# Four raw weight buffers for the whole kernel, and the first gates in bytes that are free during mLSTM: a two-layer mixer trunk on one core

## The chip, the core and the metric

The kernel runs on 1 core of one Trainium2 chip. The metric is the device time of one execution in microseconds (us). The engines are named as in the profile: PE (matmul), PEld (its weight loads), DVE (VectorE), ACT (ScalarE), POOL (GpSimd) and SP (SyncE, which issues nearly all transfers of this kernel).

## The reference

A trunk of two layers works on 768 tokens (256 context and 512 latent) of width 1024, all in float32. Cut to what matters here, one layer is:

```python
hx = modulate(rms_norm(x, ln1), shift, scale)        # the same for the context
px = split_in(hx @ w_in + b_in)                      # 12 mixer parts and 3 * 1024 gate columns
a, b, c = token_mixers(px[:12])                      # HGRN2, mLSTM, RG-LRU, both directions
g = sigmoid(px[12])                                  # (tokens, 3, 1024)
merged = sum(g[n] * (branch[n] @ w_branch[n]) for n in range(3))
x = x + mod2 * (merged @ w_out)
x = x + mod5 * swiglu(modulate(rms_norm(x, ln2), ...), w_ffn_in, w_ffn_out)
```

The modulation vectors come from `silu(c) @ w_ada + b_ada`. The context stream runs through the merge and the FFN in the first layer only, so the second layer (L1) has outputs of 512 tokens and the first (L0) of 768.

## The kernel before

**Precision and panels.** Every large matmul is made of three: a weight panel of 128 x 1024 raw float32 is loaded (`ld`, always on SP), ACT copies it to a rounded high part `wh` (line 195), DVE subtracts to get the low part `wl` (line 197), and PE multiplies wh by the high and low parts of the activations and wl by the high part. `wload` does this for all phases. The raw panels rotate through a tag `w` with 2 buffers, `wh` and `wl` through 3 each, in the pool `wp` that lives for the whole kernel. In the merge and FFN phase `panel` gives every second panel a raw buffer from another tag, `wx`, with 2 buffers in that phase's own pool, so that panels alternate between `wx` and `w`. The loads of the modulation weights (`ada_steps`, 80 of them, 512 KB each) also rotate through `w`.

**Phases.** Memory is used in phases, each with a pool laid over the bytes of the one before: `stp` (start: modulation weights, tokens, the first norm), then for each layer `M0`/`M1` (the mixers) and `B0`/`B1` (merge, output projection, FFN). The order of first request, or an explicit list (`M_ORDER`), sets the addresses of the tags in a pool. A tile waits for the users of those earlier tiles that lay on its own bytes.

**Mixer phase.** Per layer: value projections `v_half`, four `hgrn` heads, four `lru` blocks, the mLSTM gates (names `L0mg`, `L1mg`), and `mlstm(0)` and `mlstm(1)` (names `L0ml`, `L1ml`). One `mlstm` has four projections (PE line 370), a prelude (transposes, the weighted keys, the chunk states, lines 927 to 959) and a loop over the output chunks, six in L0 and four in L1. One chunk is a chain: a transfer and DVE line 971, ACT exp (line 973), PE line 977, DVE line 980, PE lines 987 and 989, then ACT and DVE lines 992 to 997. After the loop, `head_norm_out` normalises and transposes (PE line 626), and the result is stored to DRAM.

**Merge.** `gates(br, m, tiles)` multiplies the layer's input by two blocks of 128 gate columns (two panels, PE line 1032, name `L0br_acc`) and writes tanh of it (ACT line 1051) into two tiles. In L0 such a pair has 96 matmuls and takes four PSUM buffers, in L1 48 and two; the tag `acc` has four. Branch 0 comes first: four pairs of gates go to the tags `ex` and `hid`, then the mixer results are loaded back (`zt`, 2 buffers), split (`bh`, 8 buffers, lines 1069 and 1070) and multiplied by `w_branch`. Branches 2 and 1 follow, each with one pair of gates ahead of its branch matmuls, in the tag `gt` with 4 buffers:

```python
gts = gates(br, 0, [B("gt") for _ in range(2)]) if n_ else []
for m in range(0, NK, 2):
    gcur = gts if n_ else mg[m:m + 2]
```

**Order.** Each engine has one queue, in an order that is fixed when the program is built, from priorities (roughly the order of the program text) and from what is expected to be ready. Panel loads and splits have a raised priority (`hoist`) after the first two heads; PE can therefore run a later phase's matmuls between those of a chain, if their panels and PSUM buffers are there.

Of the kernel before, what the change touches and what calls it, by code (L numbers as in the profile page):

```python
# [8 lines left out]
F32 = mybir.dt.float32  # L9
# [8 lines left out]
NK = 8  # L18
CTX = 256
LAT = 512  # L20
T = CTX + LAT
# [12 lines left out]
LEVELS = (1, 2, 4, 8, 16, 32, 64)  # L34
BUFS = {
# [3 lines left out]
}  # L39
M_ORDER = (("v", 516), ("z", T), ("o", T), ("kt", T), ("ks", 384), ("F", T), ("sd", T), ("th", T), ("q", T), ("K", T), ("Q", T), ("P", 384), ("col", 384))  # L40
HOIST = 4000


# [1 line left out]
def trunk_kernel(ctx: ExitStack, tc: tile.TileContext, a: dict, out: bass.AP):  # L45
    nc = tc.nc
    PSUM = bass.MemoryType.PSUM
    const = ctx.enter_context(tc.tile_pool(name="const", bufs=1))
    hp = ctx.enter_context(tc.tile_pool(name="hp", bufs=16))
    wp = ctx.enter_context(tc.tile_pool(name="wp", bufs=2))  # L50
# [8 lines left out]
    def nm(p):  # L59
        n_names[0] += 1  # L60
        return f"{part[0]}{p}{n_names[0]}"
# [3 lines left out]
    def S(tag, n=T, dt=F32, p=128):  # L65
        return pool[0].tile([p, n], dt, tag=tag, name=nm(tag), bufs=BUFS[tag])

    def phase(name, order=()):
        st = ExitStack()
        pool[0] = st.enter_context(tc.tile_pool(name=name, bufs=1, reuse_waits="tile"))  # L70
        for tag, n in order:
            S(tag, n)
        return st
# [28 lines left out]
    def ld(o, i):  # L102
        nc.sync.dma_start(o, i)

    stp = phase("stp")
    ii, jj, xr = [S("ij", 128, I32) for _ in range(3)]
    G.iota(ii, pattern=[[0, 128]], base=0, channel_multiplier=1)
    G.iota(jj, pattern=[[1, 128]], base=0, channel_multiplier=0)
    ident = const.tile([128, 128], F32, name="ident")
    V.tensor_tensor(ident, ii, jj, op=OP.is_equal)  # L110
    ones = const.tile([128, 1], F32, name="ones")
    V.memset(ones, 1.0)
    crow = const.tile([16, 128], F32, name="crow")
    ld(crow[0:8], a["c"].rearrange("b (k p) -> (b k) p", p=128))
    ld(crow[8:16], a["c_ctx"].rearrange("(k p) -> k p", p=128))
    tokst, awt = [], {}
# [7 lines left out]
    def ada_src(l, s, j):  # L124
        return a["w_ada"][l][s * 256:(s + 1) * 256, j * 512:(j + 1) * 512].rearrange("(k p) c -> p k c", p=128)
# [68 lines left out]
    def split_w(w, n, wh, wl, low=True):  # L194
        ACT.activation(wh[:, :n], w[:, :n], AF.Copy)  # L195
        if low:
            V.tensor_tensor(wl[:, :n], w[:, :n], wh[:, :n].bitcast(F32), op=OP.subtract)  # L197

    WN = 1088

    def wload(src, r0, nk, c0, ncol, extra=None, wl=None, low=True, w=None):
        with tc.high_priority(hoist[0]):
            w = w or wp.tile([128, WN], F32, tag="w", name=nm("w"), bufs=2)
            wh = wp.tile([128, WN], F32R, tag="wh", name=nm("wh"), bufs=3)
            if wl is None:
                wl = wp.tile([128, WN], F32R, tag="wl", name=nm("wl"), bufs=3)
            cw = ncol + (extra[1] if extra else 0)
            n = nk * cw
            v = w[:, :n].rearrange("p (k c) -> p k c", k=nk)
            ld(v[:, :, :ncol], src[r0:r0 + nk * 128, c0:c0 + ncol].rearrange("(k p) c -> p k c", p=128))  # L210
            if extra:
                ld(v[:, :, ncol:], src[r0:r0 + nk * 128, extra[0]:extra[0] + extra[1]].rearrange("(k p) c -> p k c", p=128))
            split_w(w, n, wh, wl, low)
        return (wh[:, :n].rearrange("p (k c) -> p k c", k=nk), wl[:, :n].rearrange("p (k c) -> p k c", k=nk))
# [22 lines left out]
    def ada_acc(ac, kk, wv):  # L237
        for i in range(len(ac)):
            if kk == 0:
                V.tensor_scalar(ac[i], wv, csk[:, kk, i:i + 1], None, op0=OP.mult)  # L240
            else:
                V.scalar_tensor_tensor(ac[i], wv, csk[:, kk, i:i + 1], ac[i], op0=OP.mult, op1=OP.add)  # L242
# [10 lines left out]
    def ada_steps(l, js):  # L253
        for j in js:
            nv = 2 if l == 0 or j < 4 else 1
            ac = None
            for s in range(4):
                was, part[0] = part[0], f"ada{l}_{j}_"
                w = wp.tile([128, WN], F32, tag="w", name=nm("w"), bufs=2)
                wv = w[:, :1024].rearrange("p (k c) -> p k c", k=2)  # L260
                with tc.high_priority(HOIST):
                    ld(wv, ada_src(l, s, j))
                if s == 0:
                    ac = [S("ny", 512) for _ in range(nv)]
                with tc.high_priority(HOIST):
                    for k in range(2):
                        ada_acc(ac, 2 * s + k, wv[:, k, :])
                if s == 3:
                    ada_reduce(l, j, ac)
                part[0] = was  # L270
                yield
# [254 lines left out]
    for c in LEVELS:  # L526
        lt = S("lt", 128)
# [14 lines left out]
    def hbcol(l, c0):  # L542
        i = c0 // 128 if c0 < 4096 else 32 + (c0 - 4112) // 128
        return halfb[l][:, i:i + 1]
# [3 lines left out]
    def layer(l, hh, hl):  # L548
# [4 lines left out]
        no = T - t0  # L553
# [19 lines left out]

        mpool = phase(f"M{l}", M_ORDER)
        rst = S("rst", T, p=64)
# [7 lines left out]
        vb = S("vb", 512)  # L583
        ld(vb, bass.AP(tensor=a["b_in"].tensor, offset=a["b_in"][l, O_V:O_V + 512].offset, ap=[[0, 128], [1, 512]]))
        vbm = S("vbm", 528)
# [416 lines left out]
            mlstm(p)  # L1002

        mpool.close()
        bpool = phase(f"B{l}")
        XO = t0

        def B(tag, dt=F32):
            return S(tag, no, dt)

        turn = [0]

        def panel(src, r0, nk, c0, wl=None, low=True):
            turn[0] += 1
            return wload(src, r0, nk, c0, 256, wl=wl, low=low, w=S("wx", 1024) if turn[0] % 2 else None)

        def dense2(panels, ah, al, groups, ao=0, mid=None):
            nks = [p[0].shape[1] for p in panels]
# [22 lines left out]
        def kpanels(src, r0, nks, c0, wls=(None, None), low=True):  # L1041
            out_, r = [], r0
            for nk, wl in zip(nks, wls):
                out_.append(panel(src, r, nk, c0, wl, low))
                r += nk * 128
            return out_

        def gates(br, m, gts_):
            col = O_GATE + br * D + m * 128
            for mm, ps, off, n in dense2(kpanels(w_in, 0, (4, 4), col), hh, hl, OG):  # L1050
                ACT.activation(gts_[mm][:, off - XO:off - XO + n], ps, AF.Tanh, scale=0.5, bias=hbcol(l, col + mm * 128))
            return gts_
# [3 lines left out]
            filler = ada_steps(0, range(4, 10))  # L1056
        part[0] = f"L{l}br0_"
        mg = [None] * NK
        for m in (6, 0, 2, 4):
            mg[m], mg[m + 1] = gates(0, m, [B("ex" if m == 6 else "hid") for _ in range(2)])  # L1060
        mh, mlo = [], []
        for n_, (br, zs) in enumerate(((0, za), (2, zc), (1, zb))):
            part[0] = f"L{l}br{br}_"
            bh, bl = [], []
            for i in range(4):
                z = B("zt")
                ld(z, zs[i][:, OT])
                zh, zl = B("bh", F32R), B("bh", F32R)
                ACT.activation(zh, z, AF.Copy)
                V.tensor_tensor(zl, z, zh.bitcast(F32), op=OP.subtract)  # L1070
                bh.append(zh)
                bl.append(zl)
            gts = gates(br, 0, [B("gt") for _ in range(2)]) if n_ else []
            for m in range(0, NK, 2):
                gcur = gts if n_ else mg[m:m + 2]
                for mm, ps, off, n in dense2([panel(a["w_branch"][l, br], 0, 4, m * 128)], bh, bl, OG, ao=XO):
                    gt = gcur[mm]
                    sl = slice(off - XO, off - XO + n)
                    V.scalar_tensor_tensor(gt[:, sl], gt[:, sl], 1.0, ps, op0=OP.add, op1=OP.mult)  # L1079
                    if n_:  # L1080
                        V.tensor_tensor(mg[m + mm][:, sl], mg[m + mm][:, sl], gt[:, sl], op=OP.add)
                if n_ == 2:
                    for i in (m, m + 1):
                        h_, l_ = B("hid", F32R), B("hid", F32R)
                        ACT.activation(h_, mg[i], AF.Copy, scale=0.5)
                        V.scalar_tensor_tensor(l_, mg[i], 0.5, h_.bitcast(F32), op0=OP.mult, op1=OP.subtract)
                        mh.append(h_)
                        mlo.append(l_)
                        mg[i] = None
                next(filler, None)  # L1090
                next(filler, None)
                if n_ and m + 2 < NK:
                    gts = gates(br, m + 2, [B("gt") for _ in range(2)])
        for _ in filler:
            pass

# [18 lines left out]
        xn = xs if l == 0 else [S("xn", 512) for _ in range(NK)]  # L1115
# [13 lines left out]
        for off, n in (GA, GB):  # L1129
            st = Stat(n, no)  # L1130
            for m0 in range(0, NK, 2):
                for mm, ps, _, _ in dense2(kpanels(a["w_out"][l], 0, (4, 4), m0 * 128), mh, mlo, ((off, n),), ao=XO):
                    m = m0 + mm
# [14 lines left out]
        hid = {}  # L1148
# [66 lines left out]
        for off, n in (GA, GB):  # L1215
# [29 lines left out]
            else:  # L1245
# [5 lines left out]
                for c in range(2):  # L1251
                    cb_ = (off - 256) // GR + 16 * c
                    for hf in range(2):
                        o = og[c][hf]
# [40 lines left out]
```

## Time and profile before

| | us |
|---|---|
| median of 3 runs | 2728.51 |
| lowest and highest | 2722.21 and 2735.47 |
| the profiled execution, own time | 2732.03 |
| its span | 2730.3 |
| PE busy in the span | 2577.0 |

The span is what the trace covers; 1.7 us of the execution's own time lie outside it. The granted TensorE clock averaged 0.962 of full speed. Times in the rows below count from the span's start, and line numbers are those of the kernel before.

### The profile page before, as it was taken

The page shows a single profiled execution, that of the slowest core. Times are in us where ns is not written, and L with a number is a line of the kernel's source. Part 1 is how long each engine was busy: PE and PEld are TensorE (multiplying, and loading weights), DVE is VectorE, ACT ScalarE, POOL GpSimd, SP SyncE. Part 2 cuts the span into 40 slices and gives each one's busy share as a digit, 9 for nine tenths or more (in the row PEclk, how much of TensorE's full clock was granted, in tenths as well). Part 3 has the DMA queues.
Part 4 walks back from the last instruction along what each step waited for, and adds up shares of the span by engine and source line. Part 5 has one row for each costly group of instructions (what it writes and reads, how often), then busy time and mean ns, then how long its engine had stood idle before and what let it go on. Part 6 is the DMA issues. An engine that isn't in the chain of part 4 may idle for free.

```text
span 2730.3 us, 35992 instructions
## 1 busy us (share of the span) xinstructions
PE 2577.0 (94%) x14415; PEld 2209.6 (81%) x14415; DVE 1583.0 (58%) x3023; ACT 956.5 (35%) x1468; POOL 12.0 (0%) x44
## 2 busy tenths in 40 slices
PE   6999999967999999999999989999897999999998
PEld 3999878756888888888888879987775888888887
DVE  6676796452655558645545366687853445743435
ACT  3434593212122343212212245348521333422223
POOL 0000000000000000000000000000000000000000
PEclk9999999958999999999999989999996999999999
DMA  6224243216545434424434144645343555423323
GB/s 218 55 41 53 45 69 63 59 43 139 127 113 117 119 122 134 131 90 142 131 92 140 61 110 62 58 58 68 51 83 71 132 101 148 136 95 95 99 89 112
DMA packets 270168, 264.42 MB, mean 97 GB/s; under 512 B 16136, under 2 KB 233616, under 8 KB 270000
## 3 DMA queue, kind: packets, MB, share of 16 engines
q1 hardware_dynamic: 269424, 261.06, 40.4%
q8 instruction: 114, 1.87, 0.3%
q10 hardware_dynamic: 576, 1.05, 0.1%
q14 instruction: 54, 0.44, 0.1%
HBM read 249.91 MB, written 12.16 MB: 96 GB/s over the span
## 4 chain that ended last, share of the span: by engine, by line
PE 73%; DVE 11%; DMA 9%; ACT 4%; issue 2%; SPq 0%; ACTq 0%; DVEq 0%
PE L1ffn_acc L1032 13%; PE L0ffn_acc L1032 13%; PE L0br_acc L1032 10%; PE L1br_acc L1032 6%; DMA ada_w<-in_w_ada_dram 4%; PE L0hg_acc L370 4%; PE L1hg_acc L370 3%; PE L0out_acc L1032 2%; PE L0lru_acc L370 2%; DVE ada_ny L242 2%; PE L0ml_acc L370 2%; PE L0hg_pl L693 2%; PE L1ml_acc L370 1%; PE L1mg_acc L480 1%; PE L1hg_pl L693 1%
## 5 line engine op out<-in xcount | busy, mean ns | idle before, releaser
L1032 PE MATMUL L0ffn_acc<-L0out_h,L0ffn_wh 128*128 128x256 f32 (+1 forms) x1408 | 348.6, 339 | 9.1 <-DVE L0ffn_gt L1160 4.5
L1032 PEld LDWEIGHTS L0ffn_acc<-L0out_h,L0ffn_wh 128*128 128x128 f32 x1408 | 241.2, 190 | 41.7 <-DVE L0ffn_gt L1160 5.8
L1032 PE MATMUL L0ffn_acc<-L0out_h,L0ffn_wl 128*128 128x512 f32 (+1 forms) x704 | 236.5, 336 | 0.0
L242 DVE SCALAR_TENSOR_TENSOR ada_ny<-ada_w,csk,ada_ny 128x512 f32<-128x512 f32 x224 | 158.2, 748 | 126.2 <-DMA ada_w<-in_w_ada_dram 125.5
L1032 PE MATMUL L1ffn_acc<-L1out_h,L1ffn_wh 128*128 128x512 f32 (+1 forms) x736 | 219.8, 381 | 1.8 <-ACT L1out_h L360 0.9
L1032 PE MATMUL L0br_acc<-h,L0br_wh 128*128 128x512 f32 (+1 forms) x768 | 192.7, 343 | 14.8 <-ACT L0br_wh L195 10.1
L1032 PE MATMUL L0ffn_acc<-L0ffn_hid,L0ffn_wh 128*128 128x256 f32 (+1 forms) x704 | 173.5, 338 | 0.0
L1032 PEld LDWEIGHTS L0br_acc<-h,L0br_wh 128*128 128x128 f32 x768 | 134.1, 193 | 31.8 <-ACT L0br_wh L195 10.6
L1032 PEld LDWEIGHTS L1ffn_acc<-L1out_h,L1ffn_wh 128*128 128x128 f32 x736 | 136.2, 188 | 28.9 <-DVE L1out_h L361 1.5
L1032 PEld LDWEIGHTS L0ffn_acc<-L0out_h,L0ffn_wl 128*128 128x128 f32 x704 | 133.2, 189 | 14.3
L1032 PE MATMUL L1ffn_acc<-L1out_h,L1ffn_wl 128*128 128x512 f32 (+1 forms) x368 | 139.4, 380 | 0.0
L370 PE MATMUL L0hg_acc<-h,L0hg_wh 128*128 128x384 f32 (+2 forms) x512 | 136.3, 343 | 0.0
L1032 PEld LDWEIGHTS L0ffn_acc<-L0ffn_hid,L0ffn_wh 128*128 128x128 f32 x704 | 120.3, 188 | 15.6
L1032 PE MATMUL L0br_acc<-h,L0br_wl 128*128 128x256 f32 (+1 forms) x384 | 130.8, 341 | 0.0
L1032 PE MATMUL L1br_acc<-L0ffn_h,L1br_wh 128*128 128x512 f32 x384 | 119.9, 394 | 10.4 <-ACT L1br_wh L195 10.4
L1032 PE MATMUL L1ffn_acc<-L1ffn_hid,L1ffn_wh 128*128 128x512 f32 (+1 forms) x448 | 116.6, 349 | 0.0
L197 DVE TENSOR_TENSOR L1ffn_wl<-L1ffn_w,L1ffn_wh 128x1024 fp32r<-128x1024 f32 (+1 forms) x38 | 44.4, 1170 | 115.4 <-ACT L1ffn_wh L195 115.3
L195 ACT ACTIVATE L0ffn_wh<-L0ffn_w 128x1024 fp32r<-128x1024 f32 (+1 forms) x38 | 38.6, 1016 | 200.6 <-PE L0ffn_acc L1032 173.0
L370 PE MATMUL L1hg_acc<-L0ffn_h,L1hg_wh 128*128 128x384 f32 (+1 forms) x384 | 108.7, 362 | 0.0
L1032 PE MATMUL L0ffn_acc<-L0ffn_hid,L0ffn_wl 128*128 128x256 f32 (+1 forms) x304 | 102.7, 338 | 0.0
L1032 PE MATMUL L0br_acc<-L0br_bh,L0br_wh 128*128 128x512 f32 (+1 forms) x384 | 96.3, 342 | 3.9 <-DVE L0br_hid L1079 3.9
L370 PEld LDWEIGHTS L0hg_acc<-h,L0hg_wh 128*128 128x128 f32 x512 | 90.4, 189 | 4.8
(680 smaller groups left out, 5930.4 us busy)
## 6 DMA issues: line engine op xcount, KB each, us to landing
ada_w<-in_w_ada_dram SPq DMA_DIRECT2D x80, 512.0 KB
L0ffn_wx<-in_w_ffn_in_dram SPq DMA_DIRECT2D x22, 512.0 KB
L0ffn_w<-in_w_ffn_in_dram SPq DMA_DIRECT2D x22, 512.0 KB
L1ffn_wx<-in_w_ffn_in_dram SPq DMA_DIRECT2D x22, 512.0 KB
L1ffn_w<-in_w_ffn_in_dram SPq DMA_DIRECT2D x22, 512.0 KB
L0hg_w<-in_w_in_dram SPq DMA_DIRECT2D x16, 512.0 KB
L1hg_w<-in_w_in_dram SPq DMA_DIRECT2D x16, 512.0 KB
L0br_w<-in_w_in_dram SPq DMA_DIRECT2D x12, 512.0 KB
```

Of the source, the lines that this page charges most:

```text
L195: ACT.activation(wh[:, :n], w[:, :n], AF.Copy)
L197: V.tensor_tensor(wl[:, :n], w[:, :n], wh[:, :n].bitcast(F32), op=OP.subtract)
L242: V.scalar_tensor_tensor(ac[i], wv, csk[:, kk, i:i + 1], ac[i], op0=OP.mult, op1=OP.add)
L370: PE.matmul(ps[:, :n], A[:, k, :], B[k][:, off - ao:off - ao + n], start=(i == 0), stop=(i == 3 * nk - 1))
L480: PE.matmul(ps[:, :n], A[k][:, c * 128:(c + 1) * 128], W[:, k % 4, :], start=k == 0 and i == 0, stop=k == 7 and i == 3 * (k1 - k0) - 1)
L693: PE.matmul(pv[:, j * 128:(j + 1) * 128], ks[:, j * 128:(j + 1) * 128], comp(Q[g], c, j, j + 1), start=True, stop=True)
L1032: PE.matmul(ps[:, :n], A[:, k, sl], Bm[k0 + k][:, off - ao:off - ao + n], start=cnt[key] == 0, stop=cnt[key] == tot - 1)
```

## The change

The change has these parts.

1. The tag `w` has 4 buffers in `wp` for the whole kernel, and `wx` is gone: panels and modulation weights share the four. (`wp` grows by 2 x 4352 bytes per partition, the pools `B0` and `B1` shrink by 2 x 4096.)
2. `M_ORDER` is another order, and now lists all tags; `B0` and `B1` get an explicit order, `B_ORDER`. In L0 `gt` comes to lie over `P`, `rst` and `vb` and beyond the end of `M0`, and in L1 over `vbm`, `z` and `ks`: tiles that mLSTM no longer uses. `zt` and `ex` lie over `v`, `hid` over `q`, `K` and the tags after them. `ny`, which lay under the next layer's `rst` and `vb`, moves to where `kt` and `o` are.
3. Two pairs of gates of branch 2, (2, 0) and (2, 2), are written in the program ahead of branch 0's four pairs, and go to all four `gt` tiles. In branch 2 the gates then stay two pairs ahead of the branch matmuls; for branch 1 the order is as before.
4. The start's pool puts `aw` first, and `crow` moves into it from `const`.

```diff
-    "bh": 8, ... "xn": 8, "wx": 2,
-    "ij": 3, "P": 4, "rst": 1, "vb": 1, "vbm": 1, "col": 3, "ex": 2, "zt": 2,
+    "bh": 8, ... "xn": 8,
+    "ij": 3, "crow": 1, "P": 4, "rst": 1, "vb": 1, "vbm": 1, "col": 3, "ex": 2, "zt": 2,
-M_ORDER = (("v", 516), ("z", T), ("o", T), ("kt", T), ("ks", 384), ("F", T), ("sd", T), ("th", T), ("q", T), ("K", T), ("Q", T), ("P", 384), ("col", 384))
+M_ORDER = (("v", 516), ("q", T), ("K", T), ("F", T), ("th", T), ("Q", T), ("kt", T), ("o", T), ("sd", T), ("col", 384),
+           ("vbm", 528), ("z", T), ("ks", 384), ("P", 384), ("rst", T), ("vb", 512))
+B_ORDER = ("zt", "ex", "hid", "ny", "bh", "xn", "gt")
...
-    stp = phase("stp")
+    stp = phase("stp", (("aw", 1024),))
...
-    def wload(src, r0, nk, c0, ncol, extra=None, wl=None, low=True, w=None):
+    def wload(src, r0, nk, c0, ncol, extra=None, wl=None, low=True):
         with tc.high_priority(hoist[0]):
-            w = w or wp.tile([128, WN], F32, tag="w", name=nm("w"), bufs=2)
+            w = wp.tile([128, WN], F32, tag="w", name=nm("w"), bufs=4)
...
-        bpool = phase(f"B{l}")
+        bpool = phase(f"B{l}", [(t, 512 if t == "ny" else no) for t in B_ORDER if l or t != "xn"])
...
         def panel(src, r0, nk, c0, wl=None, low=True):
-            turn[0] += 1
-            return wload(src, r0, nk, c0, 256, wl=wl, low=low, w=S("wx", 1024) if turn[0] % 2 else None)
+            return wload(src, r0, nk, c0, 256, wl=wl, low=low)
...
+        early = [gates(2, m, [B("gt") for _ in range(2)]) for m in (0, 2)]
         for m in (6, 0, 2, 4):
             mg[m], mg[m + 1] = gates(0, m, [B("ex" if m == 6 else "hid") for _ in range(2)])
...
-            gts = gates(br, 0, [B("gt") for _ in range(2)]) if n_ else []
+            if n_ == 2:
+                early = [gates(br, 0, [B("gt") for _ in range(2)])]
             for m in range(0, NK, 2):
-                gcur = gts if n_ else mg[m:m + 2]
+                gcur = early.pop(0) if n_ else mg[m:m + 2]
...
-                if n_ and m + 2 < NK:
-                    gts = gates(br, m + 2, [B("gt") for _ in range(2)])
+                nxt = m + 2 * len(early) + 2
+                if n_ and nxt < NK:
+                    early.append(gates(br, nxt, [B("gt") for _ in range(2)]))
```

## Rows read from the trace of the kernel before

**Rows 1.** The page, part 1: busy time by engine.
```profile
PE 2577.0 (94%) x14415; PEld 2209.6 (81%) x14415; DVE 1583.0 (58%) x3023; ACT 956.5 (35%) x1468; POOL 12.0 (0%) x44
```

**Rows 2.** Windows of L0: length, busy by engine (instructions), PE clock, DMA share, GB/s.
```profile
500.00:550.00 50.00, 49.84 (x280) 39.54 (x277) 27.75 (x98) 14.62 (x37) 0.00 (x0) 0.96 0.15 41
550.00:564.00 14.00, 7.56 (x60) 5.86 (x60) 10.83 (x29) 2.44 (x5) 0.00 (x0) 0.69 0.50 138
564.00:604.00 40.00, 33.26 (x100) 23.18 (x99) 13.44 (x56) 8.15 (x26) 0.00 (x0) 0.50 0.07 20
604.00:625.00 21.00, 3.06 (x12) 2.29 (x12) 8.49 (x22) 3.06 (x6) 0.00 (x0) 0.50 0.46 116
625.00:650.00 25.00, 20.25 (x97) 16.86 (x98) 8.32 (x8) 7.20 (x10) 0.00 (x0) 0.84 0.73 116
```

**Rows 3.** Timeline of PE in L0: start, length, work, idle before and its releaser.
```profile
522.64 0.48 PE L987 MATMUL L0ml_mx<-L0mg_v,L0ml_Q 128*128 128x129 f32 x2
...
529.07 0.49 PE L987 MATMUL L0ml_mx<-L0mg_v,L0ml_Q 128*128 128x129 f32 x2
...
589.14 0.80 PE L987 MATMUL L0ml_mx<-L0mg_v,L0ml_Q 128*128 128x129 f32 x2 [2.59 <-DVE L0ml_Q L980]
...
598.04 0.80 PE L987 MATMUL L0ml_mx<-L0mg_v,L0ml_Q 128*128 128x129 f32 x2 [2.59 <-DVE L0ml_Q L980]
...
625.05 1.22 PE L1032 MATMUL L0br_acc<-h,L0br_wh 128*128 128x512 f32 x2 [10.15 <-ACT L0br_wh L195]
```

**Rows 4.** Timeline of SP's queue at the end of L0's mixers.
```profile
613.73 2.29 SPq L103 DMA_DIRECT2D st_d<-L0ml_K  x2
616.12 1.02 SPq L103 DMA_DIRECT2D L0br_wx<-in_w_in_dram  x2
```

**Rows 5.** The chain that ended last, in order of time: merged pieces of the merges.
```profile
743.25 50.34 PE L0br_acc L1032 x288
...
2123.14 175.89 PE L1br_acc L1032 x766
```

**Rows 6.** Windows of L1, columns as in the group of L0.
```profile
2045.00:2080.00 35.00, 29.90 (x116) 21.16 (x116) 16.57 (x59) 6.16 (x19) 0.00 (x0) 0.58 0.15 39
2080.00:2097.00 17.00, 1.94 (x8) 1.57 (x8) 5.82 (x18) 1.56 (x3) 0.00 (x0) 0.50 0.49 114
2097.00:2123.00 26.00, 24.85 (x98) 19.32 (x98) 8.45 (x9) 8.44 (x12) 0.00 (x0) 0.91 0.77 124
```

**Rows 7.** Waits: who waited for whom, us in total, times, longest.
```profile
PE L1br_acc L1032 <- ACT L1br_wh L195: 10.4, 2, 10.2
...
PE L0v_acc L480 <- DVE st_v L595: 7.2, 1, 7.2
...
PE L1v_acc L480 <- DVE L0ffn_v L595: 2.1, 1, 2.1
...
DVE ada_ny L242 <- DMA ada_w<-in_w_ada_dram: 125.5, 55, 6.7
```

**Rows 8.** Tile L0br_wx: its splits, duration ns min/median/max, first and last start.
```profile
L195 ACT ACTIVATE L0br_wh<-L0br_wx x18: 1041/1060/1064, 623.9 to 913.5; 128x1024 fp32r<-128x1024 f32 x18
L197 DVE TENSOR_TENSOR L0br_wl<-L0br_wx,L0br_wh x18: 1216/1222/1226, 625.0 to 914.6; 128x1024 fp32r<-128x1024 f32 x18
```

**Rows 9.** Timeline of SP's queue at the start.
```profile
40.41 18.84 SPq L103 DMA_DIRECT2D L0hg_w<-in_w_in_dram  x3
59.30 0.57 SPq L103 DMA_DIRECT2D st_vb<-in_b_in_dram  x1
```

**Rows 10.** Timeline of ACT where branch 2 follows branch 0, L0 and L1.
```profile
741.21 1.59 ACT L1069 ACTIVATE L0br_bh<-L0br_zt 128x768 fp32r<-128x768 f32 x2 [11.96 <-PE L0br_acc L1032]
...
752.57 0.85 ACT L1069 ACTIVATE L0br_bh<-L0br_zt 128x768 fp32r<-128x768 f32 x1 [5.59 <-DMA L0br_zt<-st_d]
...
2164.84 1.34 ACT L1069 ACTIVATE L1br_bh<-L1br_zt 128x512 fp32r<-128x512 f32 x2 [2.44 <-PE L1br_acc L1032]
...
2169.45 1.28 ACT L1069 ACTIVATE L1br_bh<-L1br_zt 128x512 fp32r<-128x512 f32 x2 [1.44 <-DMA L1br_zt<-L0ffn_d]
```

More of the change, by code (lines that the diff above doesn't have):

```diff
@@ L103, in ld @@
         nc.sync.dma_start(o, i)
-    stp = phase("stp")
+    stp = phase("stp", (("aw", 1024),))
     ii, jj, xr = [S("ij", 128, I32) for _ in range(3)]
+    crow = S("crow", 128, p=16)
     G.iota(ii, pattern=[[0, 128]], base=0, channel_multiplier=1)
@@ L112, in trunk_kernel @@
     V.memset(ones, 1.0)
-    crow = const.tile([16, 128], F32, name="crow")
     ld(crow[0:8], a["c"].rearrange("b (k p) -> (b k) p", p=128))
@@ L258, in ada_steps @@
                 was, part[0] = part[0], f"ada{l}_{j}_"
-                w = wp.tile([128, WN], F32, tag="w", name=nm("w"), bufs=2)
+                w = wp.tile([128, WN], F32, tag="w", name=nm("w"), bufs=4)
                 wv = w[:, :1024].rearrange("p (k c) -> p k c", k=2)
@@ L1009, in B @@
             return S(tag, no, dt)
-        turn = [0]
         def panel(src, r0, nk, c0, wl=None, low=True):
-            turn[0] += 1
-            return wload(src, r0, nk, c0, 256, wl=wl, low=low, w=S("wx", 1024) if turn[0] % 2 else None)
+            return wload(src, r0, nk, c0, 256, wl=wl, low=low)
         def dense2(panels, ah, al, groups, ao=0, mid=None):
```

2 rows, old and new, of the table BUFS are left out of this document.

## The prediction, made before the changed kernel ran

> **What bounds the kernel now.** I read the page first. PE is busy 2577 of 2730 us [rows 1], so the time is that of PE's stream, and what can be won is its idle time (153 us) and the time that it runs at half clock. Then I cut the span into windows to find where these lie. Most of them are flat: PE full, clock 1.00. The dead time gathers where a layer's mixers end and its merge begins. In L0 PE is busy 33.3 of 40 us in the chunk loop of the second mLSTM at a granted clock of 0.50 (1.2 of 2.4 GHz), and then 3.1 of 21 us [rows 2]; L1 shows the same in its last 78 us before the merge runs steadily [rows 6]. The window before shows what is missing. In 500 to 550 the loop of the first mLSTM runs, with the projections of the second between its matmuls: 49.8 of 50 us busy, clock 0.96 [rows 2]. The timeline gives the pace of a chunk as the distance between equal matmuls: 6.43 us with that filling, 8.90 us without, at half clock, with 2.59 us idle in front of each [rows 3]. The second loop has nothing to fill it, since branch 0's first gate panel goes to a `wx` buffer, and its load stands in SP's queue behind the stores that end mLSTM [rows 4]. So PE waits another 10.15 us for its split in L0 [rows 3] and 10.2 in L1 [rows 7].
>
> **The clock, row and rule.** The loop stayed at 0.50 although PE was busy most of it [rows 2], after a prelude with idle time (7.6 of 14 us busy); filled, the same loop had 0.96. The Trainium skill's TensorE: Matmul & The Clock Gate (Part 1) says that the slow clock is the default and that matmul activity lifts it. Read simply, the loop would have lifted its own clock; the trace doesn't show that. By the rule the filling would win only idle time, and the L0 term below would be some 13 us smaller (33.3 busy us against 20.0 at full clock); that gives some 2670, inside the forecast's own spread, and has one part in five of its chance. I go by the rows.
>
> **The unit.** Gates cost PE the same wherever they run. In L0's steady merge 288 matmuls take 50.34 us, 0.175 each, so a pair of 96 takes 16.8 us; in L1 766 take 175.89, 0.230 each, so a pair of 48 takes 11.0 [rows 5]. The two early pairs are 33.6 us of filling in L0 and 22.0 in L1. They add nothing: branch 2 has that much less later.
>
> **L0, mixers to merge.** A matmul of the loop is recorded with 0.48 us filled and 0.80 at half clock [rows 3], a factor 0.60. Full-clock work from 550 to 650 is then 7.56 x 0.69 = 5.2, 33.26 x 0.60 = 20.0, 3.06 x 0.60 = 1.8, and the 97 merge matmuls that had run by 650, 17.0: 44 of 100 us, so 56 are dead [rows 2].
> With the change the panels come through `w`, which asks nothing of the mixers' pool, so loads and splits can run ahead. Six chunks at the filled pace are 38.6 us against about 40, so I leave the end of the mLSTM chain where it was: PE's last transposes ended at 625.05 - 10.15 = 614.9 [rows 3]. Up to there PE has 64.9 - 27.0 = 37.9 us for gates, enough for both pairs.
> *Most:* both are done by 614.9, and gates go on without a gap. Before, 17.0 us of gates were done at 650. The gain is 35.1 + 33.6 - 17.0 = 51.7.
> *Less:* a pair needs all four `acc` buffers in L0. If ACT's evictions stand behind its mLSTM work, one pair fills the loop and the second waits: 35.1 + 16.8 - 17.0 = 34.9.
> *Least:* nothing fills, but the panels are there when mLSTM ends: the wait of 10.15.
> The two filled cases are both open; I take 42, near their middle.
> Moved with the gates are, in each layer, four panel loads on SP and four splits, 1.06 us each on ACT and 1.22 on DVE [rows 8], 4.2 and 4.9 in all. They are free while ACT (8.2 of 40 us busy) and DVE (13.4 of 40) have room in the loop [rows 2]; if they all fell on the chain, they would take 9.1 us off the gain. On SP they pass the small mLSTM loads. The evictions stand among ACT's mLSTM steps; a late one holds the next chunk's exp, and that holds DVE line 980 and PE.
>
> **L1, the same.** Work at full clock from 2045 to 2097 is 29.90 x 0.60 = 17.9 and 1.94 x 0.60 = 1.2; the 98 merge matmuls to 2123 are 22.5 [rows 6]. PE's last transposes ended about 2097 - 10.2 = 2086.8 [rows 7]. Up to there 41.8 - 19.1 = 22.7 us are free, enough for the 22.0 of both pairs, which fit the four `acc` buffers together. Most: 36.2 + 22.0 - 22.5 = 35.7. If the clock stays low, only the idle 5.1 + 4.9 us can be filled: 36.2 + 10.0 - 22.5 = 23.7. Least: 10.2. I take 29.
>
> **Four raw buffers at the start.** SP stood 18.84 us at the third `hg_w` load, waiting for one of two buffers, and the bias load `vb` was behind it [rows 9]. DVE's first additions waited for that transfer and PE for their PSUM: 7.2 us [rows 7]. Third and fourth loads now have buffers; I take 7 (0 if `vb` still stands late, 9 with some clock).
>
> **Addresses.** `vb` of L1 lay under `ny`, which the last norm uses to its end; now it lies under `gt`, free some 15 us sooner by the program. PE's wait there is 2.1 us [rows 7]: I take 2 (0 to 3). `P` and `rst` ease too, but only POOL waits for them; the other new neighbours of `zt`, `ex` and `hid` are free by mLSTM's end or its stores, before the early gates are through: nothing, as long as these gates cover them.
>
> **What it takes away.** Before, gates (2, 0) ran between branch 0's last matmul and branch 2's first, and hid the conversion of branch 2's inputs: 741.2 to 753.4, 12.2 us in L0, and 2164.8 to 2170.7, 5.9 us in L1 [rows 10]. `zt` has two buffers, so the second half of the inputs is loaded only after the first is split. Now a branch matmul comes next. Bounds: 0, if gates (2, 4) are pulled forward, to 12 and 6. PE's first 12 matmuls take the four inputs one after another and cover part, so I take -5 and -3.
>
> **`ada_steps` in four shared buffers.** DVE waited 125.5 us for these transfers [rows 7], mostly off PE's path, which stays full there. More buffers let them start sooner; panels lose their own two. I take 0, between -8 and +8, the same again as the conversions' loss, since no row shows four shared buffers.
>
> **Sum.** 42 + 29 + 7 + 2 - 5 - 3 + 0 = 72. From the profiled execution's own 2732.0 that leaves 2660.0. This execution was 3.5 us above the median of the runs, so I say 2656.5.
>
> **Rivals.** *Everything comes:* 51.7 + 35.7 + 9 + 3 with no loss is 99, 2629 against the median. For it: the first mLSTM was filled so well [rows 2]; against: four PSUM buffers in L0, and the conversions. 15%.
> *The gates don't fill the loop:* PE's order, fixed beforehand, keeps them behind mLSTM. Then 10.15 + 10.2 + 7 + 2 - 8 = 21 are left, 2707. For it: in L0 nothing of the merge pool ran before the mixers' stores, even where its bytes were free [rows 4]; against: these matmuls write PSUM alone, and the first loop's filling did the same. 18%.
> *The ring starves panels, slower:* 80 modulation loads now queue for the buffers that panels had for themselves. DVE's mean wait for one is 125.5 / 55 = 2.3 us [rows 7]. Passed on to PE by half of them, that is 92 us, 20 more than the 72, 2748. It decides from 0.9 us per load on. Against it: three split panels stand between a raw buffer and PE, 3 x 48 matmuls or 25 us of its work in L0. 9%.
> *No gain to be measured:* the order at the turn changes, but other waits take the place of all. 2725. 6%.
> My forecast has 52%.
>
> **How the numbers follow.** Timing can tell some 0.5% (13.6 us) from no change. The range 2620 to 2710 holds the forecast's own spread (2635 to 2680 from the bounds of its terms), the full gain and most of the unfilled case; it leaves out the slower case, the no-gain case and a few per cent of the tails. Faster has the forecast, the full gain and two thirds of the unfilled case: 0.80. Same: 0.10. Slower: 0.10.
>
> **What would show it.** Right: gate matmuls of branch 2 on PE between lines 987 and 989 of the second mLSTM, its clock near 1.00 and its pace near 6.4 us; no 10 us wait for a split at the merge's start; PE's idle time down by some 50 us. Wrong: a loop still at 0.50; early gates in a block after the last transposes; a gap of over 6 us between branches 0 and 2; PE waiting for splits while DVE waits for `ada_w`.

## The result and the profile after

The changed kernel takes 2650.18 us (median of 4 runs, 2647.65 to 2653.56) against 2727.95 of the kernel before: ratio 0.9714, 95% interval 0.9687 to 0.9741. The prediction was 2656.5. The profiled execution has 2653.56 us and a span of 2651.8, 78.5 less than before. PE does the same 14415 matmuls; its idle time fell from 153 to 100 us, and the granted clock rose from 0.962 to 0.982. This line of the page answers to [rows 1]; up to the merge all line numbers are now two higher.

```profile
PE 2551.9 (96%) x14415; PEld 2190.0 (83%) x14415; DVE 1585.0 (60%) x3023; ACT 956.7 (36%) x1468; POOL 11.8 (0%) x44
```

Where the time went is read from the first and last matmul of each tile on PE. This cuts the two spans at the same work (lengths in us):

| stage | before | after | gained |
|---|---|---|---|
| start to the last projection of L0's second mLSTM | 549.7 | 549.7 | 0.0 |
| L0: from there to the first matmul of the output projection | 398.1 | 360.2 | 37.9 |
| L0: output projection and FFN | 653.7 | 653.9 | -0.2 |
| L1: value projection, to the first `hgrn` matmul | 36.5 | 30.8 | 5.7 |
| L1: from there to the last projection of the second mLSTM | 404.9 | 395.2 | 9.7 |
| L1: from there to the output projection | 256.0 | 230.6 | 25.4 |
| L1: the rest | 431.4 | 431.4 | 0.0 |

**L0.** Windows of the changed kernel, to be held against [rows 2] (length; busy of PE, PEld, DVE, ACT, POOL with instructions; granted clock; DMA share; GB/s). The last two are L1, against [rows 6]:

```profile
545.40:589.60 44.20, 43.62 (x274) 34.29 (x272) 29.03 (x89) 12.11 (x31) 0.00 (x0) 1.00 0.37 99
589.60:609.80 20.20, 9.27 (x33) 6.82 (x33) 11.47 (x33) 6.39 (x14) 0.00 (x0) 0.58 0.29 27
...
1989.80:2031.00 41.20, 38.80 (x200) 26.94 (x199) 23.22 (x66) 10.64 (x24) 0.00 (x0) 0.99 0.46 98
2031.00:2041.80 10.80, 10.80 (x40) 8.59 (x40) 6.33 (x20) 3.33 (x6) 0.00 (x0) 0.73 0.37 35
```

The loop is full at clock 1.00 for 44 us, and then dead again for 20: 9.27 us of work at 0.58. PE's timeline shows where the filling ends, at 590:

```profile
589.62 0.39 PE L1031 MATMUL L0br_acc<-h,L0br_wl 128*128 128x256 f32 x1
...
593.35 0.77 PE L989 MATMUL L0ml_mx<-L0mg_v,L0ml_Q 128*128 128x129 f32 x2 [3.00 <-DVE L0ml_Q L982]
...
606.72 1.52 PE L628 MATMUL L0ml_mx<-ident,L0ml_o 128*128 128x128 f32 x6 [7.51 <-DVE L0ml_o L623]
...
609.85 1.20 PE L1031 MATMUL L0br_acc<-h,L0br_wh 128*128 128x512 f32 x2
```

96 gate matmuls, one pair of L0, ran in the loop. The second pair starts at 609.85, right behind the transposes and without the 10.15 us wait of [rows 3]. ACT's timeline says what held it (line 975 is the exp of the last chunk, lines 994 and 998 end a chunk, line 617 is in the head's norm, line 1050 is the gates' tanh):

```profile
590.57 1.05 ACT L197 ACTIVATE L0br_wh<-L0br_w 128x1024 fp32r<-128x1024 f32 x1
591.51 0.62 ACT L975 ACTIVATE L0ml_Q<-L0ml_Q 128x512 f32<-128x512 f32 x1
596.67 0.17 ACT L994 ACTIVATE L0ml_mrd<-L0ml_mx 128x2 f32<-128x2 f32 x1 [4.54 <-PE L0ml_mx L991]
...
601.48 0.84 ACT L617 ACTIVATE L0ml_K<-L0ml_o 128x768 f32<-128x768 f32 x1 [1.02 <-DVE L0ml_o L999]
602.23 1.98 ACT L1050 ACTIVATE L0br_gt<-L0br_acc,halfb 128x512 f32<-128x512 f32 x4
```

The pair's last matmul ended at 590.4 and ACT was idle for 4.54 us, but the four tanh stand behind line 617, mLSTM's last step on ACT. They end at 604.2; until then all four `acc` buffers are held, and PE's order has the second pair behind the transposes. SP's queue, against [rows 4], has the gate panels ahead of mLSTM's stores now:

```profile
552.98 0.37 SPq L105 DMA_DIRECT2D L0br_w<-in_w_in_dram  x1
...
592.90 0.37 SPq L105 DMA_DIRECT2D L0br_w<-in_w_in_dram  x1
609.01 2.29 SPq L105 DMA_DIRECT2D st_d<-L0ml_K  x2
```

**The turn from branch 0 to branch 2**, against [rows 10]. PE waits three times in L0 (1.35 us for the modulation's sums that run there, 0.28 and 3.34 for the inputs of branch 2) and once in L1:

```profile
733.20 1.25 PE L250 MATMUL ada_pl<-ident,ada_ny 128*128 128x128 f32 x8 [1.35 <-DVE ada_adas L252]
734.73 0.51 PE L1031 MATMUL L0br_acc<-L0br_bh,L0br_wh 128*128 128x512 f32 x1 [0.28 <-DVE L0br_bh L1070]
741.86 1.62 PE L1031 MATMUL L0br_acc<-L0br_bh,L0br_wh 128*128 128x512 f32 x5 [3.34 <-ACT L0br_bh L1069]
...
2112.69 0.50 PE L1031 MATMUL L1br_acc<-L1br_bh,L1br_wh 128*128 128x512 f32 x1 [1.15 <-ACT L1br_bh L1069]
```

**The start**, against [rows 9]. SP now runs two panel loads further ahead and then stands at the fifth, which waits 9.2 us for DVE's split of the first panel; `vb` is still behind it:

```profile
40.37 16.33 SPq L105 DMA_DIRECT2D L0hg_w<-in_w_in_dram  x5
56.76 0.57 SPq L105 DMA_DIRECT2D st_vb<-in_b_in_dram  x1
57.42 5.42 SPq L105 DMA_DIRECT2D st_vbm<-in_b_in_dram  x2
```

Two groups of the waits answer to [rows 7]. PE's wait for the first additions is longer than before (9.4 for 7.2), DVE's for modulation weights is shorter (79.2 for 125.5); that of PE for `vb` in L1 is gone, and so are both 10 us waits for a split.

```profile
PE L0v_acc L482 <- DVE st_v L597: 9.4, 1, 9.4
DVE ada_ny L244 <- DMA ada_w<-in_w_ada_dram: 79.2, 41, 5.0
```

### The profile page after: what moved, and what is told of

It reads as the page before. It is cut to its first block, busy times and chain, and to the rows that moved or that the text cites. A ratio compares the mean times of both kernels' runs of the same rounds, so it can differ in the third digit from the quotient of the medians.

```text
span 2651.8 us, 36000 instructions
## 1 busy us (share of the span) xinstructions
PE 2551.9 (96%) x14415; PEld 2190.0 (83%) x14415; DVE 1585.0 (60%) x3023; ACT 956.7 (36%) x1468; POOL 11.8 (0%) x44
## 4 chain that ended last, share of the span: by engine, by line
PE 52%; DVE 4%; DMA 2%; ACT 1%; issue 1%; SPq 0%; ACTq 0%; DVEq 0%
PE L0ffn_acc L1031 18%; PE L1ffn_acc L1031 14%; PE L1br_acc L1031 7%; PE L1hg_acc L372 4%; PE L1mg_acc L482 1%; PE L1lru_acc L372 1%; PE L1hg_pl L695 1%; PE L1ml_acc L372 1%; PE L1out_acc L1031 1%; PE L1v_acc L482 1%; PE L1lru_pl L795 1%; DMA L1ml_Q<-L1mg_d 1%; PE L1ml_mx L991 0%; DVE L0ffn_h L363 0%; PE L1ml_mx L989 0%
## 5 line engine op out<-in xcount | busy, mean ns | idle before, releaser
L1031 PE MATMUL L0ffn_acc<-L0out_h,L0ffn_wl 128*128 128x256 f32 (+1 forms) x704 | 237.3, 338 | 0.0
L244 DVE SCALAR_TENSOR_TENSOR ada_ny<-ada_w,csk,ada_ny 128x512 f32<-128x512 f32 x224 | 157.7, 748 | 80.3 <-DMA ada_w<-in_w_ada_dram 79.2
L197 ACT ACTIVATE L0ffn_wh<-L0ffn_w 128x1024 fp32r<-128x1024 f32 (+1 forms) x76 | 77.2, 1015 | 279.4 <-PE L0ffn_acc L1031 251.9
L199 DVE TENSOR_TENSOR L1ffn_wl<-L1ffn_w,L1ffn_wh 128x1024 fp32r<-128x1024 f32 (+1 forms) x76 | 88.8, 1169 | 143.0 <-ACT L1ffn_wh L197 142.3
L197 ACT ACTIVATE L1ffn_wh<-L1ffn_w 128x1024 fp32r<-128x1024 f32 (+1 forms) x76 | 77.2, 1015 | 199.8 <-PE L1ffn_acc L1031 159.1
L199 DVE TENSOR_TENSOR L0ffn_wl<-L0ffn_w,L0ffn_wh 128x1024 fp32r<-128x1024 f32 (+1 forms) x68 | 81.0, 1191 | 110.3 <-ACT L0ffn_wh L197 109.8
L1031 PE MATMUL L1ffn_acc<-L1out_h,L1ffn_wl 128*128 128x512 f32 (+1 forms) x368 | 139.4, 380 | 0.0
```

The costliest lines, as they stand in the source:

```text
L1031: PE.matmul(ps[:, :n], A[:, k, sl], Bm[k0 + k][:, off - ao:off - ao + n], start=cnt[key] == 0, stop=cnt[key] == tot - 1)
```

## The experiments

The profile raised a question: 96 gate matmuls ran in the loop, but their tanh came behind mLSTM. So, it seemed, neither the bytes of `gt` nor which gates come first had mattered to them. The first four runs take the change apart. Theory A is the prediction's credit: the early gates in free bytes fill the loop. Theory B says that the four raw buffers (called the ring below) do it alone, since the matmuls of any first gate pair write only PSUM.

**Old order of gates** (all other parts of the change kept):

```diff
-        early = [gates(2, m, [B("gt") for _ in range(2)]) for m in (0, 2)]
...
-            if n_ == 2:
-                early = [gates(br, 0, [B("gt") for _ in range(2)])]
+            gts = gates(br, 0, [B("gt") for _ in range(2)]) if n_ else []
```

> The changed kernel with the gates in the old order: branch 0's four pairs first, branch 2's first pair after branch 0's matmuls. Four raw buffers and the new layout stay. Theory A (the gates that are written first, in bytes free during mLSTM, fill the loop): the second mLSTM loop is empty again, granted clock near 0.50, only the 10 us split waits stay away; of the 38 us (L0) and 32 us (L1) about 10 each are left, 2695 to 2705 us. Theory B (the panels' own raw buffers are what counts; any first gate pair fills, since its matmuls write PSUM alone): the same number of gate matmuls runs in the loops, now of branch 0, clock near 1.00, and the gap between branches 0 and 2 (5 us in L0, 5 in L1) closes, 2638 to 2652 us.

Measured: 2634.14 us, 16 below the changed kernel and 4 below the range of theory B (ratio 0.9656 to before, 0.964 to 0.9671). The same 96 matmuls fill the loop, now of branch 0.

**The ring alone** (the kernel before, four `w`, no `wx`, and `crow` moved):

```diff
-            w = w or wp.tile([128, WN], F32, tag="w", name=nm("w"), bufs=2)
+            w = wp.tile([128, WN], F32, tag="w", name=nm("w"), bufs=4)
...
-            return wload(src, r0, nk, c0, 256, wl=wl, low=low, w=S("wx", 1024) if turn[0] % 2 else None)
+            return wload(src, r0, nk, c0, 256, wl=wl, low=low)
```

> The kernel before with only four w buffers in place of two w and two wx (and the 512 bytes of crow moved, without which it has no room): old orders of addresses, gates in the old order. Theory A: 10 us per layer from the split waits, nothing from filling, 2700 to 2710 us. Theory B: loops filled as in the changed kernel, no gap at branch 2; lost against the changed kernel only the 5 to 8 us at the start of L1, which come from the address of vb: 2640 to 2658 us. Should the start of L1 be as quick as in the changed kernel, that gain is the ring's too and not the address's.

Measured: 2631.02 us (0.9645, 0.9631 to 0.9659), below the range that either theory gave. Its windows of L0, from the last projection to the last transposes and from there to the output projection:

```profile
546.10:605.30 59.20, 48.14 (x275) 36.88 (x274) 36.56 (x110) 18.49 (x44) 0.00 (x0) 0.87 0.27 76
605.30:896.80 291.50, 291.50 (x1683) 256.83 (x1681) 170.54 (x250) 75.22 (x97) 0.00 (x0) 1.00 0.50 126
```

The whole merge of L0 runs without a gap. The start of L1 is as quick as in the changed kernel (29.9 us), though all addresses follow the old rule: with `wx` gone, what follows it in the pool moves, and `vb` is issued 10.7 us after the FFN's end (10.2 in the changed kernel, 25.2 before).

**The old rule for addresses** (early gates and ring kept):

```diff
-M_ORDER = (("v", 516), ("q", T), ("K", T), ...
+M_ORDER = (("v", 516), ("z", T), ("o", T), ...
...
-        bpool = phase(f"B{l}", [(t, 512 if t == "ny" else no) for t in B_ORDER if l or t != "xn"])
+        bpool = phase(f"B{l}")
```

> The changed kernel with the old rule for addresses in the mixers' and the merge's pools (gt now comes first and lies on v, which mLSTM's stages before use; no list of lifetimes). Four buffers and the early gates stay. If the free bytes are what lets the early gates run (theory A): the tanh waits for its bytes, the second half of the loop is slower, 2665 to 2700 us. Theory B: the tanh stands behind mLSTM's last step on ACT in either layout, so both merges take the same time to 2 us, and only the start of L1 may lose 5 to 8 us: 2648 to 2660 us.

Measured: 2651.04 us, as the changed kernel. `gt` lies on `v` here, and its tanh still starts right behind mLSTM's last step on ACT, the second of these lines:

```profile
603.12 0.84 ACT L615 ACTIVATE L0ml_K<-L0ml_o 128x768 f32<-128x768 f32 x1 [1.02 <-DVE L0ml_o L997]
603.87 1.98 ACT L1048 ACTIVATE L0br_gt<-L0br_acc,halfb 128x512 f32<-128x512 f32 x4
```

The start of L1 takes 34.6 us here, 3.8 more than in the changed kernel: `vb` is late again (23.4 us after the FFN's end) and PE waits 3.1 us for it. The second mLSTM of L1, from its last projection to its last transposes, takes 48.3 us and not 52.0. L0's merge is 3.0 us shorter here. So the new layout gives and takes about the same.

**`wx` again, with early gates and the new layout:**

```diff
-    "bh": 8, "hid": 16, "gt": 4, ...
+    "bh": 8, "hid": 16, "wx": 2, "gt": 4, ...
...
-B_ORDER = ("zt", "ex", "hid", "ny", "bh", "xn", "gt")
+B_ORDER = ("wx", "zt", "ex", "hid", "ny", "bh", "xn", "gt")
...
+            return wload(src, r0, nk, c0, 256, wl=wl, low=low, w=S("wx", 1024) if turn[0] % 2 else None)
```

> The changed kernel with the panels of merge and FFN again alternating between two wx buffers in the phase's own pool (over v) and two w. Early gates and the layout stay. Theory A with order as the cause: early gates still fill, 2650 to 2665 us. Theory B: the first panel's load stands behind mLSTM's stores again, loops at clock 0.50, splits awaited for 10 us in each layer, and the gap at branch 2 stays, so about the time before, 2715 to 2740 us.

Measured: 2723.89 us (0.9983, 0.9973 to 0.9994), in the range of theory B. Its window of the loop, SP's queue behind it and PE's wait there are of the same kind as before, the wait 7.8 us for 10.15:

```profile
551.00:616.00 65.00, 44.79 (x171) 32.36 (x171) 31.83 (x105) 12.74 (x36) 0.00 (x0) 0.53 0.15 44
```

```profile
615.28 2.29 SPq L105 DMA_DIRECT2D st_d<-L0ml_K  x2
617.68 1.02 SPq L105 DMA_DIRECT2D L0br_wx<-in_w_in_dram  x2
```

```profile
624.27 1.22 PE L1034 MATMUL L0br_acc<-h,L0br_wh 128*128 128x512 f32 x2 [7.81 <-ACT L0br_wh L197]
```

Not one gate matmul is in the loop. Theory A has fallen. Whether `wx` is late by its pool or by its bytes is not told apart: it lies over `v` in both kernels that have it, and the loop reads `v` until 602.8 us before and 604.1 here. The load came some 13 us after that, since SP stood at the stores of mLSTM (27.9 us before); a `wx` on free bytes was not run. The four runs and the changed kernel make a table (medians):

| | old rule for addresses | new layout |
|---|---|---|
| ring, gates in the old order | 2631.0 | 2634.1 |
| ring, early gates | 2651.0 | 2650.2 |
| `wx` in the merge's pool | 2728 (old order) | 2723.9 (early gates) |

The ring is worth 97 us; the new layout costs between -1 and 3, and the early gates *cost* 16 to 20.

**Two buffers.** Is it the number of buffers, or the pool? The kernel before without `wx` and with two `w` for all:

```diff
-            return wload(src, r0, nk, c0, 256, wl=wl, low=low, w=S("wx", 1024) if turn[0] % 2 else None)
+            return wload(src, r0, nk, c0, 256, wl=wl, low=low)
```

> The kernel before with wx taken away and nothing put in its place: all panels and modulation weights share two w buffers, all orders and addresses by the old rules. Theory B1 (what counts is that the panel's raw buffer doesn't lie in a pool that opens behind the mixers; the number doesn't matter): both mLSTM loops are filled as with four, gate matmuls in them, clock near 1.00, 2630 to 2660 us. Theory B2 (four buffers are needed so that loads run ahead): PE waits for splits through merge and FFN, since 80 modulation loads share the two; from 0.5 us per panel of the 230 on it would lose 115 us, so 2700 us or slower, above the kernel before if 0.4 us per panel are lost.

Measured: 2671.90 us (0.9799, 0.9781 to 0.9817), between the ranges of the two theories. Half the raw buffers, and still 57 us faster than before; so of the ring's 97 us some 57 come with `wx` gone and some 41 with the number. The loop of L0 is filled (first window). The profile's span is 41.7 us longer than with four: 4.8 by the end of that loop, 12.9 in L0's merge (second window) and 26.4 in L1, less 2.4 in L0's output projection and FFN.

```profile
547.50:610.10 62.60, 48.84 (x274) 37.23 (x273) 36.52 (x110) 18.50 (x44) 0.00 (x0) 0.87 0.35 68
610.10:914.50 304.40, 297.29 (x1683) 260.94 (x1682) 167.36 (x250) 74.72 (x97) 0.00 (x0) 0.98 0.48 121
```

**Cover at the turn.** What do the early gates cost? A third pair, where the old kernel had its first, in two tiles of `hid`:

```diff
+            if n_ == 1:
+                early.append(gates(br, 4, [B("hid") for _ in range(2)]))
```

> The changed kernel with a third pair of gates ahead, (2, 4), written where the old kernel had (2, 0): between branch 0 and branch 2, in two tiles of hid. If the gap at that turn (PE idle 5.0 us between 727 and 744 us in L0, 5 in L1) is the price of the missing cover, it closes and the time falls by 6 to 10 us, to 2640 to 2645 us. If the gap comes from transfers that would be late anyway, PE waits after the pair instead and the time stays within 3 us of 2650.

Measured: 2638.44 us (0.9677, 0.9658 to 0.9696), 12 below the changed kernel and 1.6 below the range expected. The first line is this run's merge of L0, the second the same stretch of the changed kernel:

```profile
609.50:900.50 291.00, 291.00 (x1682) 256.69 (x1681) 168.99 (x250) 75.10 (x97) 0.00 (x0) 1.00 0.48 127
```

```profile
609.80:909.90 300.10, 295.09 (x1682) 258.55 (x1681) 168.54 (x250) 75.34 (x97) 0.00 (x0) 0.99 0.47 123
```

The difference is 9.1 us in L0: 5.0 idle, and 4.1 in which PE is busy longer with as many matmuls. Of the 4.1, 1.1 lie ahead of the turn: the first 682 matmuls take 119.9 us and 118.8 with cover, the clock being 0.83 for 0.97 from 610 to 620. So the turn costs 8.0 us. In L1's merge the difference is 1.8.

**The tiles of the first gates in a pool that opens before the second mLSTM.** Theory C: the place of the tanh in ACT's order follows the pool of its tile, not the bytes. `P`, `rst` and `vb` get a pool at the other end of the memory (`rp`), which closes between the two `mlstm` calls, and `gt` a pool that opens there (both through a new helper, `right`):

```diff
         for p in range(2):
+            if p == 1:
+                rp.close()
+                gp = right(f"G{l}", (("gt", no),))
             mlstm(p)
```

> The changed kernel with P, rst and vb in a pool of their own at the other end of the memory, which closes between the two mLSTM calls, and gt in a pool that opens there. So gt belongs no longer to a pool that opens behind mLSTM. Theory C (the early pair's tanh stands behind mLSTM's last step on ACT only because its tile's pool opens there, and the second pair then waits for PSUM): the tanh moves into the loop, some 70 more gate matmuls run before the last transposes (12.6 us at 0.175), the 7.5 us wait of the head norm is filled. Also vb of L0 is no longer behind the fifth panel load, so the 9.4 us wait at the start falls to between 0 and 5. Together 2626 to 2638 us. If PE's order or DVE's chain is the limit: L0's merge starts as late as in the changed kernel, 2641 to 2650 us.

Measured: 2627.71 us (0.9639, 0.962 to 0.9657), 22 below the changed kernel and in the range of theory C. The tanh of the first pair now stand in the loop, and 168 gate matmuls run before the last transposes. ACT's timeline (two of four) and the window of the loop:

```profile
566.55 0.69 ACT L1064 ACTIVATE L0br_gt<-L0br_acc,halfb 128x512 f32<-128x512 f32 x1 [0.31 <-PE L0br_acc L1045]
...
584.68 0.46 ACT L1064 ACTIVATE L0br_gt<-L0br_acc,halfb 128x256 f32<-128x256 f32 x1
```

```profile
546.50:604.40 57.90, 57.53 (x347) 45.46 (x345) 37.74 (x111) 20.94 (x47) 0.00 (x0) 1.00 0.37 77
```

At the start `vb` is now ahead of the panel loads, at 29.74 us. PE's 9.4 us wait for it is gone, and the first projection of `hgrn` starts 7.2 us earlier (67.7 for 74.9). But the first matmul behind these projections starts only 1.3 us earlier (107.5 for 108.8), and that is not clear of the spread: 107.6 to 111.6 in the runs with `vb` late, 108.7 in the last run, where `vb` is early too. In place of the wait PE stops twice at the transposes of the constants, whose loads stand behind the same fifth panel. The first stop is for such a load; for the second the profile shows no releaser:

```profile
67.49 0.27 PE L187 MATMUL L0v_pl<-ident,L0v_vst 56*128 56x56 f32 x1 [1.67 <-DMA L0v_vst<-in_b_ada_dram]
...
78.81 0.25 PE L187 MATMUL L0v_pl<-ident,L0v_vst 64*128 64x64 f32 x1 [4.01 <-issue]
```

**All that helped:** ring, gates in the old order, `P`, `rst`, `vb` in their own pool, and `ex` (the first pair's tiles) in the pool that opens before the second mLSTM.

> Four buffers, gates in the old order (branch 0 first, cover at the turn kept), P, rst and vb in their own pool as in the run beside it, and ex, the tiles of the first pair, in the pool that opens there between the two mLSTM calls. By theories B and C: 2634 (the run without early gates), less 10 to 13 for the second pair in L0's loop, less 4 to 9 at the start: 2612 to 2622 us. If C is wrong, 2625 to 2634 us from the start alone.

Measured: 2616.28 us (0.9591, 0.9573 to 0.961), in the range of theories B and C, 34 us below the changed kernel and the best of all. Loop and merge of L0:

```profile
545.30:603.20 57.90, 57.58 (x347) 45.54 (x346) 37.65 (x111) 20.59 (x46) 0.00 (x0) 1.00 0.30 87
603.20:881.10 277.90, 277.90 (x1611) 245.15 (x1610) 169.34 (x249) 73.09 (x95) 0.00 (x0) 1.00 0.51 131
```

## Why the prediction was right, and where it was not

**The bound and the mechanism** held. The loss did sit between mixers and merge, and it came from the raw buffer of the first gate panel: put back into the merge's pool, it takes the loop's filling and its clock away and brings a wait for a split back in both layers, 7.8 us each. What was wrong is the credit. The prediction let two early pairs in free bytes fill the loop; with the ring any first pair does, and the early order loses 16 to 20 us of what the ring wins. That the sum of 72 came near the 78.5 measured is in part luck: 7 us forecast at the start did not come, and 15.4 came in L1 ahead of its second mLSTM (5.7 at the start, 9.7 in the mixers), where the sum had 2.

**L0, 42 less 5, measured 37.9.** Of the two filled cases it was the one-pair case, for the reason given there: ACT's evictions stood behind its mLSTM work, and a pair holds all four `acc` buffers. That case said 34.9 by 650 us. Measured are 316 gate matmuls by 650, where before there were 97: 219 x 0.175 = 38.3. The excess goes with mLSTM's chain, which I left where it was: its last transposes end at 609.8, 4.7 us earlier than before. The merge before lost another 3.9 us idle after 650, and some 3.6 at a lower clock behind that stop (0.96 from 650 to 743: 496 instructions in 89.1 us, 85.5 at the pace after 743). I counted neither. The turn costs 8.0, where I took 5 between 0 and 12. So 38.3 + 7.5 - 8.0 = 37.8: that 42 less 5 came so near is luck with terms that were each some microseconds off.

**L1, 29 less 3, measured 25.4.** Here both pairs fit: 96 gate matmuls are in the window before the last transposes, at 0.99 of the clock to the end of the chunk loop. From the last transposes on 33.4 us are won (212.0 before, 178.6 now). But these transposes come 52.0 us after the last projection, 44.0 before: I left the end of the chain where it was, and that was 8.0 wrong. PE is busy in 49.6 of the 52.0; with four buffers and the old addresses the stretch takes 48.3 (early gates) and 48.4 (old order), so the new layout has a part in it. The turn takes 1.2 us idle, 1.8 by the run with cover.

**The start, 7, measured 0.** This step failed. I had a buffer for the third and fourth load and did not ask for the fifth: SP's order has it ahead of `vb` as well. The third load of two buffers and the fifth of four wait for the same event, DVE's split of the first panel (it ends at 58.9 before and 56.3 now), so `vb` is issued at 59.3 and at 56.8. I also misread [rows 9]: the 18.84 us span three issues, and the wait for that split in them is 10.9. And the size was wrong too: with `vb` moved ahead, 1.3 us or nothing come, as the constants are late next.

**Addresses, 2, measured 5.7 at the start of L1.** `vb` gave the 2.1 of its wait. Some 2.3 more are PE's wait for the norm's sums (line 338, now 340): 3.1 before and 3.6 with `wx` put back, but 0.8 or less in every run without `wx`, with two `w` as with four. So it goes with `wx`; by what path I have not traced.

**`ada_steps`, 0, measured -0.2** in the output projection and FFN of L0, where most of these loads are. The slower rival, a ring that starves panels, did not come: DVE's wait for the weights fell.

**Not in the sum: 9.7 us in L1's mixers.** Runs with four buffers take 391.4 to 397.5 us for this stage, the kernel before 404.9, and the two other runs with two `w` 396.5 and 401.5. So the buffers are likely, but the ranges overlap, and which load is late in which wait I have not traced.

**The clock.** One loop of one kernel shows both sides: filled it ran at 1.00, and when the filling ended it fell to 0.58 over the last 20 us. In the run with all that helped the same stretch (590.3 to 603.2) keeps 1.00. The Trainium skill's TensorE: Matmul & The Clock Gate (Part 1) says that matmul activity lifts the clock; by the simple reading of it the L0 stage would have gained some 13 us less, 25. The trace does not bear that reading out: the last chunk, with a stop of 3.00 us in front, ran at half clock again, and before the change the clock stayed at 0.50 from 563.6 to 578.8 us with PE busy in 15.1 of these 15.2.

**Early gates' cost, the rest.** The run with cover gives 12 of the 16 us back. The profiles of the changed kernel and of the old order of gates differ by 19.6: 8.0 in L0's merge, 2.2 in L1's, 3.0 up to L0's last projection and 6.4 in small pieces. Part of it is in L0's mLSTM: from its first to its last projection it takes 109.3 to 111.2 us in the four runs with ring and early gates and 105.3 to 106.9 in the three with four buffers and the old order. There DVE waits for the loads of `K`, 8.0 to 8.2 us in the four and 5.8 to 6.1 in the three; the lines are the changed kernel's and the old order's. Why these loads take longer is not settled.

```profile
495.48 0.17 DVE L943 COPY L0ml_mdec<-L0ml_K 128x6 f32<-128x6 f32 x1 [8.16 <-DMA L0ml_K<-L0mg_d]
```

```profile
494.55 0.17 DVE L943 COPY L0ml_mdec<-L0ml_K 128x6 f32<-128x6 f32 x1 [5.83 <-DMA L0ml_K<-L0mg_d]
```

## What to carry to other kernels

Before you reorder work to fill a gap, ask in which pool each buffer of that work lives: raw buffers in the pool of the next phase kept 96 matmuls out of the loop, and its clock at 0.53, though the gates were written first. Where work is brought forward, look at what it covered in its old place, and leave a cover there. A stall that is removed from a queue shows its value only after the next late transfer is known: here 9.4 us of waiting were worth 1.3 at most.

## What the runs showed that I had not expected

- Free bytes did not bring a tile's first write forward. With `gt` on free bytes and on `v`, the tanh stood in the same place, behind mLSTM's last step on ACT (602.23 and 603.87 us); in a pool that opened earlier, its first was at 566.55. How the order comes about when the program is built, no run shows.
- Two raw buffers that live for the whole kernel (2671.9 us) beat four of which two belong to the merge (2728).
- A turn with 5.0 us of idle time cost 8.0 us of the stage: from it on as many matmuls were busy 3.0 us longer, and from 740 to 750 the granted clock was 0.83 for 1.00.
